# Heads 6 and 7 of the last branch in the tiles of x rows, the output's seventh operand loaded early, x rows added in the first pair, and the last addition ahead of the division

## The chip, the cores and the metric

One core of one Trainium2 chip. The time is the device time of one execution in microseconds (us). The core has five engines that run their own instruction streams: TensorE (PE in the profile, its weight loads PEld), VectorE (DVE), ScalarE (ACT), GpSimd (POOL) and SyncE (SP), which here issues nearly all DMA. An engine waits for another, or for a DMA, at a semaphore.

## What is computed

One layer that mixes 2048 tokens of width 1024 (float32), cut to its end, which is what the change touches:

```python
merged = jax.nn.sigmoid(g_a) * (y_a @ w_pa) + jax.nn.sigmoid(g_b) * (y_b @ w_pb)   # y_b: 8 heads x 128
out_x  = merged @ w_out + b_out
x      = x + gate[:, None, :] * out_x
return rmsnorm(x, g_final)
```

Ahead of it stand a projection of x, a gated convolution that gives y_a, and a bidirectional mLSTM scan of 8 heads that gives y_b.

## The kernel before

**Splits.** Every float32 factor of a large product is split in two, a high part (a cast, on ScalarE) and a low part (raw minus high, a subtraction, on VectorE). A product is three passes of matmuls: high by high, high by low, low by high. `split` (L177 to L182: the cast is L178, the subtraction L179) does it.

**Stages.** The tokens are worked on in two halves of T = 1024. At the end of the program come four branches, in this order: `w_pa` and `w_pb` for the second half, `w_pa` for the first half, beside which the last heads of the scan are finished, and `w_pb` for the first half. This text calls the last of them the last branch. A branch is eight slabs, one for each 128 columns of the weight; a slab sums 8 heads (k = 0 to 7) in three passes for two halves (j) of 512 tokens. In slab 0 both halves are run head by head; from slab 1 on one half is finished before the other. After a slab, `PbEnd.end` gates the sum (L1518), adds the part of `w_pa` on POOL (L1519) and writes it to a DRAM array `mgd` (L1520). `mgd` is read again as weights of the output.

**Heads of a branch.** `Branch.fetch` loads a head from DRAM (`ybd`) straight into the tile of its low part, lets some steps pass, and splits it there. Its `region` says where the tiles lie: region 0 takes x slots 0 to 15; region 1, which the last branch uses before the change, takes x slots 16 to 27 for heads 0 to 5 and eight small slots (`u`, `cv` in rows of the trace) for heads 6 and 7, in two halves. Heads 0 to 2 were fetched early; each later head is fetched when its scan is done.

**Output.** `output` runs eight pairs (m = 0 to 7). A pair takes 256 rows of tokens and multiplies their 1024 columns of `mgd` with `w_out` in seven products (operands o = 0 to 6 of `wod`, made earlier) into five PSUM banks, in the order X Y X W Z V Z. An operand is 12 matmuls, a pair 84. So the seventh operand uses bank Z a second time, and its first matmul must wait until the fifth operand's sum has been taken out of Z. `fin` takes sums out: into a tile `xt` of a row block of x, to which POOL has added the bias row `gb` (L1580, in `begin`), it adds an earlier part `u` (L1604) and the bank (L1605, on VectorE). For a row block with both halves, ScalarE has its squares (L1607), POOL its reciprocal root `sx` (L1611, L1613, L1614), and `close` multiplies by `sx` and the row `gf` (L1596) and writes it out. The weights of the pairs, sums of blocks of `mgd` (`sw`, made on POOL, L360), are split on the way.

The operands o = 4, 5, 6 are loaded at the start of `output` (L1626), and their six halves split inside the first pair, at steps 20, 26, 32, 40, 46 and 52 of its 84. x rows of pairs 0, 1, 2 are loaded and added to `gb` in the last branch, those of pair m + 2 at step 34 of pair m. `gb`, `gf`, and the six tiles `xt` lie in a pool `so`, which is opened where the scan's pool `sp_` is released.

**Order of the work.** TensorE's order is that of the program text. The instructions wrapped in `pin` keep their place on their engine; the other instructions of VectorE, ScalarE, POOL and SP are put in order by a scheduler. `run(...)` interleaves a stage with the queued generators `urgent` and `later`, so many steps of these for each matmul.

Of the kernel before, what the change touches and what calls it, by code (L numbers as in the profile page):

```python
# [11 lines left out]
FR = mybir.dt.float32r  # L12
# [6 lines left out]
P = 128  # L19
# [22 lines left out]
def hybrid_kernel(ctx: ExitStack, tc, x, c, ctxt, c_ctx, w_ada, b_ada, g_norm, w_in, b_in,  # L42
# [1411 lines left out]
    class Branch:  # L1454
# [11 lines left out]
        def fetch(self, k, wait=12):  # L1466
            if self.region == 0 or k < 6:
                base = 2 * k if self.region == 0 else 16 + 2 * k
                hi, lo = [xslot(base + p, [P, T], FR) for p in range(2)]
                parts = [(hi, lo, self.raw(k))]  # L1470
                for p, t in enumerate((hi, lo)):
                    for j in range(2):
                        self.t[p, k, j] = t[:, S2[j]]
            else:
                slots = [uslot] * 3 + [vslot] * 5
                parts = []
                for j in range(2):
                    hi, lo = [slots[4 * (k - 6) + 2 * j + p](FR) for p in range(2)]
                    parts.append((hi, lo, self.raw(k)[:, S2[j]]))
                    self.t[0, k, j], self.t[1, k, j] = hi, lo  # L1480
            for _, lo, raw in parts:
                ld.dma_start(lo.bitcast(F32), raw)
            yield from gap(wait)
            for hi, lo, _ in parts:
                split(hi, lo, lo.bitcast(F32), pinned=wait > 0)
# [54 lines left out]
    yb = Branch(1, lambda k: ybd[0][k], ())  # L1540
    urgent.extend(yb.fetch(k, 24) for k in ready)

    def heads_done(h):
        urgent.append(yb.fetch(h))
# [38 lines left out]
    urgent.extend(load_wo(o) for o in range(4))  # L1583
    urgent.extend(begin(m, 6) for m in range(3))
    run(branch(w_pb, yb, PbEnd, 0), 0, 0.35)
    flush(urgent)

    def output():
# [10 lines left out]
        def fin(m):  # L1599
            def f(i, j, ps, add):  # L1600
# [4 lines left out]
                nc.vector.tensor_tensor(xt[:, s], xt[:, s], ps, op=OP.add)  # L1605
# [10 lines left out]
                if m + 1 == len(tiles):  # L1616
                    close()
# [4 lines left out]
        wo.claim(range(4, 7))  # L1622
        for o in range(4, 7):
            for q in range(2):
                hi, lo = (wo.t[o][p][q] for p in range(2))
                ld.dma_start(lo.bitcast(F32), wod[wo.PLACE[o], :, 2 * q:2 * q + 2, :])  # L1626
                parts.append((hi, lo))
        for m in range(len(tiles)):
            for n, _ in enumerate(pair(st, wo, fin(m))):
                if m == 0 and n in (20, 26, 32, 40, 46, 52):  # L1630
                    hi, lo = parts.pop(0)
                    split(hi, lo, lo.bitcast(F32), pinned=True)
                if n in (10, 28):
                    close()
                if n == 34 and m > 0:
                    for _ in begin(m + 2):
                        pass
# [32 lines left out]
```

## Time and profile before

| | us |
|---|---|
| median of 3 runs | 2660.72 (2659.01 to 2660.84) |
| the profiled execution, its own time | 2660.47 |
| its span | 2658.7 |
| TensorE busy in the span | 2594.5 (98%) |
| VectorE, GpSimd, ScalarE busy | 1722.6 (65%), 1123.8 (42%), 1099.0 (41%) |
| last branch, from its first matmul to the first of the output | 2397 to 2485 of the span |

The span runs from the first to the last instruction that the profiler recorded; the time holds 1.8 us more around it. A row of a timeline gives the start, the length, the engine, the line, the operation with its tiles (out<-in), how many stand together, and in brackets the idle time of the engine ahead of it with what ended it.

### The profile page before, as it was taken

The numbers are of one execution on the slowest core, as the hardware profiler recorded it, in microseconds if no ns is written. First come the engines' busy times: TensorE is split into PE (matmuls) and PEld (weight loads), VectorE is DVE, ScalarE is ACT, GpSimd is POOL, SyncE is SP. The second block draws the span as 40 slices with busy tenths as digits, with TensorE's granted clock in tenths as the row PEclk, the third lists the DMA queues.
The fourth block names the chain that finished last, engine by engine and source line by source line (L and its number), as shares of the span: only waits on it lengthen the run. The fifth ranks groups of instructions, "written<-read, shape, count | busy, mean of one in ns | idle before, by whom it ended". The sixth has DMA issues, their size and how long they took to land.

```text
span 2658.7 us, 38177 instructions
## 1 busy us (share of the span) xinstructions
PE 2594.5 (98%) x12807; PEld 2166.7 (81%) x12807; DVE 1722.6 (65%) x3119; ACT 1099.0 (41%) x2269; POOL 1123.8 (42%) x1322
## 2 busy tenths in 40 slices
PE   8999999999999999999999999999999999999998
PEld 7788887888878787877887888888888888888777
DVE  6643237687776777478578577667666656554597
ACT  5433344333333335344443444344444544442233
POOL 1221223233345553235555555565555124422674
PEclk9999999999999999999999999999999999999999
DMA  8333344655734457435644653653566978768542
GB/s 231 101 101 106 106 139 131 211 167 179 232 118 123 139 145 236 118 100 159 195 142 130 201 160 120 195 174 128 154 195 201 301 219 273 253 194 288 195 159 96
DMA packets 373217, 452.99 MB, mean 170 GB/s; under 512 B 24428, under 2 KB 273948, under 8 KB 373020
## 3 DMA queue, kind: packets, MB, share of 16 engines
q1 hardware_dynamic: 372784, 450.46, 54.4%
q8 instruction: 102, 1.67, 0.3%
q14 instruction: 95, 0.78, 0.1%
q10 hardware_dynamic: 236, 0.08, 0.0%
HBM read 319.42 MB, written 131.03 MB: 169 GB/s over the span
## 4 chain that ended last, share of the span: by engine, by line
PE 48%; DVE 3%; DMA 2%; issue 1%; POOL 1%; ACT 0%; SPq 0%; DVEq 0%; POOLq 0%; ACTq 0%
PE pd L427 29%; PE pd L474 11%; PE pn L891 2%; PE pn L892 2%; PE pa L834 1%; PE pu L658 1%; DMA mgd<-t2k 1%; DVE wl L179 1%; PE pa L849 1%; PE pn L658 0%; PE pa L669 0%; DVE xt L1596 0%; DVE xt L1605 0%; DMA x<-wod 0%; DVE cv L999 0%
## 5 line engine op out<-in xcount | busy, mean ns | idle before, releaser
L427 PE MATMUL pd<-x,wh 128*128 128x512 f32 x5320 | 1695.9, 397 | 15.9 <-DVE xt L1605 8.5
L427 PEld LDWEIGHTS pd<-x,wh 128*128 128x128 f32 x5320 | 985.1, 189 | 209.9 <-issue 19.4
L427 PE MATMUL pd<-x,wl 128*128 128x512 f32 x2660 | 1057.3, 397 | 0.0
L427 PEld LDWEIGHTS pd<-x,wl 128*128 128x128 f32 x2660 | 501.8, 189 | 99.3 <-issue 0.2
L178 ACT CAST wh<-sw 128x512 fp32r<-128x512 f32 x382 | 237.0, 620 | 492.9 <-PE pd L427 409.0
L179 DVE TENSOR_TENSOR wl<-sw,wh 128x512 fp32r<-128x512 f32 x382 | 303.2, 795 | 182.0 <-ACT wh L178 177.1
L178 ACT CAST wh<-wr 128x512 fp32r<-128x512 f32 x350 | 216.6, 619 | 375.3 <-PE pd L427 269.9
L360 POOL TENSOR_TENSOR sw<-wr,sw 128x512 f32<-128x512 f32 x95 | 136.1, 1433 | 432.6 <-DVE wl L179 345.2
L179 DVE TENSOR_TENSOR wl<-wr,wh 128x512 fp32r<-128x512 f32 x350 | 289.7, 828 | 42.5 <-ACT wh L178 39.1
L474 PE MATMUL pd<-x,wh 128*128 128x512 f32 x896 | 281.7, 396 | 0.0
L360 POOL TENSOR_TENSOR sw<-wr 128x512 f32<-128x512 f32 x95 | 130.9, 1378 | 236.9 <-DVE wl L179 236.0
L653 POOL TENSOR_SCALAR vw<-tk,wk 128x129 f32<-128x129 f32 x205 | 161.9, 794 | 120.2 <-PE pn L658 109.7
L474 PEld LDWEIGHTS pd<-x,wh 128*128 128x128 f32 x896 | 166.3, 188 | 32.1
L474 PE MATMUL pd<-x,wl 128*128 128x512 f32 x448 | 173.4, 397 | 0.0
L186 POOL TENSOR_SCALAR ssq<-ssq 128x1 f32<-128x1 f32 x128 | 37.2, 291 | 293.7 <-ACT hf L906 289.8
L926 DVE TENSOR_TENSOR t2k<-pd,u 128x512 f32<-128x512 f32 x168 | 115.5, 688 | 59.8 <-PE pd L427 59.1
L360 POOL TENSOR_TENSOR sw<-sw,wr 128x512 f32<-128x512 f32 x94 | 132.4, 1408 | 47.9 <-DVE wl L179 37.4
L904 ACT ACTIVATE hf<-pn,rd 128x128 f32<-128x128 f32 x128 | 47.0, 367 | 246.9 <-DVE rd L900 222.4
L360 POOL TENSOR_TENSOR sw<-wr,wr 128x512 f32<-128x512 f32 x94 | 132.2, 1406 | 20.2 <-DVE wl L179 10.8
L820 POOL TENSOR_SCALAR_AFFINE_SELECT mw<-mw 128x256 f32<-128x256 f32 x128 | 61.7, 503 | 119.5 <-DMA mw<-mwd 89.1
L891 PE MATMUL pn<-tk,pt 128*128 128x129 f32 x512 | 98.8, 275 | 5.0 <-DVE hb L905 5.0
L891 PEld LDWEIGHTS pn<-tk,pt 128*128 128x128 f32 x512 | 86.8, 190 | 16.2 <-issue 5.8
(259 smaller groups left out, 3317.5 us busy)
## 6 DMA issues: line engine op xcount, KB each, us to landing
wr<-in_w_in_dram SPq DMA_DIRECT2D x176, 512.0 KB, 4.1
tk<-tokd SPq DMA_DIRECT2D x64, 386.0 KB, 3.6
mw<-mwd SPq DMA_DIRECT2D x44, 512.0 KB, 5.3
qkd<-t2k SPq DMA_DIRECT2D x64, 256.0 KB, 2.9
qk<-qkd SPq DMA_DIRECT2D x64, 256.0 KB, 3.8
tk<-tokd SPq DMA_DIRECT2D x48, 257.0 KB, 2.9
tokd<-t2k SPq DMA_DIRECT2D x32, 258.0 KB, 2.9
x<-in_w_ada_dram SPq DMA_DIRECT2D x16, 512.0 KB, 6.4
```

Source lines behind the costliest of these rows:

```text
L178: a = nc.scalar.copy(hi, raw)
L179: b = (eng or nc.vector).tensor_tensor(lo, raw, hi.bitcast(F32), op=OP.subtract)
L186: nc.gpsimd.tensor_scalar(dst, ss, 1.0 / n, EPS, op0=OP.mult, op1=OP.add)
L360: nc.gpsimd.tensor_tensor(s, a, b, op=op)
L427: nc.tensor.matmul(ps[b], op[wi][:, kk, :], xs.at(o, xi, kk), start=(fresh and kk + pi == 0), stop=(o == last[b] and kk == 3 and pi == 2), ...
L474: nc.tensor.matmul(pss[j], ops[k // 4][wi][:, k % 4, :], y(xi, k, j), start=(k + pi == 0), stop=(k == NK - 1 and pi == 2))
L653: pin(nc.gpsimd.tensor_scalar(vw, tk[:, VT], wk, None, op0=OP.mult))
L820: pin(nc.gpsimd.affine_select(mws[m][:, :, 0, d, :], mws[m][:, :, 0, d, :], pattern=[[0, 2], [s, P]], base=0, channel_multiplier=-s, compa ...
L891: nc.tensor.matmul(pn[:, d, :], pt[:, d, :], tk[:, VT], start=True, stop=False)
L892: nc.tensor.matmul(pn[:, d, :], qw[:, d, :], cur if d == carried else tk[:, ST], start=False, stop=True)
L904: nc.scalar.activation(hf, pn[:, 0, 0:P], AF.Copy, scale=rd[:, 0:1])
L926: nc.vector.tensor_tensor(t, ps, add, op=OP.add)
```

## The change

There are four edits.

1. The last branch uses a region 2. Heads 0 to 3 lie in x slots 16 to 23, heads 4 and 5 in the eight small slots, and heads 6 and 7 whole (128x1024) in tiles of the tag `xt`, that is, where x rows will lie. These two are fetched only where `so` is open, behind `gb` and `gf`.
2. With x slots 24 to 27 free, the seventh operand (o = 6) is loaded and split with operands 0 to 3 beside the last branch. In the first pair only four halves are left to split, at steps 18, 24, 32 and 40.
3. x rows: only those of pair 0 are loaded in the last branch; pair 1's at step 44 of pair 0, pair 2's at step 8 of pair 1, the others at step 36. They are stepped through `coming`.
4. In the last pair the division of a row block (`close`) is written behind the next addition of `fin`, and L1605 is pinned. The rate of the last branch's helpers is 0.36 for 0.35.

```diff
         def fetch(self, k, wait=12):
-            if self.region == 0 or k < 6:
-                base = 2 * k if self.region == 0 else 16 + 2 * k
-                hi, lo = [xslot(base + p, [P, T], FR) for p in range(2)]
+            whole = (NK, 6, 4)[self.region]
+            if k < whole or self.region == 2 and k > 5:
+                if k < whole:
+                    base = 2 * k if self.region == 0 else 16 + 2 * k
+                    hi, lo = [xslot(base + p, [P, T], FR) for p in range(2)]
+                else:
+                    hi, lo = [so.tile([P, T], FR, tag="xt", name=nm("xk"), bufs=6) for _ in range(2)]
...
-                    hi, lo = [slots[4 * (k - 6) + 2 * j + p](FR) for p in range(2)]
+                    hi, lo = [slots[4 * (k - whole) + 2 * j + p](FR) for p in range(2)]
...
-    yb = Branch(1, lambda k: ybd[0][k], ())
+    yb = Branch(2, lambda k: ybd[0][k], ())
     urgent.extend(yb.fetch(k, 24) for k in ready)
 
     def heads_done(h):
-        urgent.append(yb.fetch(h))
+        if h < 6:
+            urgent.append(yb.fetch(h))
...
-    urgent.extend(load_wo(o) for o in range(4))
-    urgent.extend(begin(m, 6) for m in range(3))
-    run(branch(w_pb, yb, PbEnd, 0), 0, 0.35)
+    last_heads = [yb.fetch(6, 6), yb.fetch(7, 1)]
+    for f in last_heads:
+        next(f)
+    urgent.extend(last_heads)
+    urgent.extend(load_wo(o) for o in (0, 1, 2, 3, 6))
+    urgent.append(begin(0, 6))
+    run(branch(w_pb, yb, PbEnd, 0), 0, 0.36)
...
-                nc.vector.tensor_tensor(xt[:, s], xt[:, s], ps, op=OP.add)
+                pin(nc.vector.tensor_tensor(xt[:, s], xt[:, s], ps, op=OP.add))
+                if m + 1 == len(tiles):
+                    close()
...
-                if m + 1 == len(tiles):
+                if m + 1 == len(tiles) and (i, j) == (0, 1):
                     close()
...
-        wo.claim(range(4, 7))
-        for o in range(4, 7):
+        wo.claim((4, 5))
+        for o in (4, 5):
...
+        coming = deque()
         for m in range(len(tiles)):
             for n, _ in enumerate(pair(st, wo, fin(m))):
-                if m == 0 and n in (20, 26, 32, 40, 46, 52):
+                if m == 0 and n in (18, 24, 32, 40):
...
-                if n == 34 and m > 0:
-                    for _ in begin(m + 2):
-                        pass
+                if (m, n) in ((0, 44), (1, 8)) or m > 0 and n == 36:
+                    coming.append(begin(len(xts), 16))
+                step(coming)
                 yield
```

In the changed file the lines below the first edit stand 4 to 11 further down: L1482 is L1486, L1580 is L1585, L1596 is L1605, L1604 and L1605 are L1613 and L1614.

The instructions move as follows. SP at the start of the last branch, before: `ybd<-g` writes head 7, the two `cv<-ybd` read it.

```order
L852 DMA ybd_135<-g_5885_23848 128x512
L252 DMA x_6023_24497<-wod 128x1024
L1503 DMA mad<-t2k_24315 128x512
L1482 DMA cv_24348<-ybd_135 128x512
L1482 DMA cv_24350<-ybd_135 128x512
L1554 DMA gb<-rowd 128x1024
L1555 DMA gf<-in_g_final_dram 128x1024
```

The same place of SP after; the tiles `xk` are heads 6 and 7.

```order
L852 DMA ybd_135<-g_5885_23848 128x512
L252 DMA x_6026_24517<-wod 128x1024
L1507 DMA mad<-t2k_24315 128x512
L1559 DMA gb<-rowd 128x1024
L1560 DMA gf<-in_g_final_dram 128x1024
L1486 DMA xk_24360<-ybd_135 128x1024
L1486 DMA xk_24363<-ybd_135 128x1024
L1517 DMA t2k_24475<-sbd_141 128x512
```

The reading loads have changed places with `gb` and `gf`, and are two whole heads instead of the halves of one.

POOL at the end of the last branch and in the first pair, before: the `t2k` rows are the branch's last gated sums, `sw` are sums of the output's weights, `sx` the first scalar operation on pair 0's rows.

```order
L1580 TENSOR_TENSOR xt_24895<-xt_24895,gb 128x1024
L1580 TENSOR_TENSOR xt_24898<-xt_24898,gb 128x1024
L1519 TENSOR_TENSOR t2k_24890<-t2k_24890,t2k_24889 128x512
L1519 TENSOR_TENSOR t2k_24930<-t2k_24930,t2k_24929 128x512
L1519 TENSOR_TENSOR t2k_24962<-t2k_24962,t2k_24961 128x512
L1519 TENSOR_TENSOR t2k_24994<-t2k_24994,t2k_24993 128x512
L360 TENSOR_TENSOR sw_25133<-wr_25027,sw_25037 128x512
L360 TENSOR_TENSOR sw_25184<-wr_25033,wr_25086 128x512
L360 TENSOR_TENSOR sw_25186<-sw_25184,wr_25033 128x512
L360 TENSOR_TENSOR sw_25233<-wr_25033 128x512
L1611 TENSOR_SCALAR sx_24811<-sx_24811 128x1
```

And after; `xt_25139` and `xt_25142` are pair 1's rows, `xt_25241` and `xt_25244` pair 2's.

```order
L1523 TENSOR_TENSOR t2k_24988<-t2k_24988,t2k_24987 128x512
L360 TENSOR_TENSOR sw_25121<-wr_25021,sw_25031 128x512
L360 TENSOR_TENSOR sw_25174<-wr_25027,wr_25074 128x512
L360 TENSOR_TENSOR sw_25176<-sw_25174,wr_25027 128x512
L1585 TENSOR_TENSOR xt_25139<-xt_25139,gb 128x1024
L1585 TENSOR_TENSOR xt_25142<-xt_25142,gb 128x1024
L360 TENSOR_TENSOR sw_25225<-wr_25027 128x512
L1622 TENSOR_SCALAR sx_24911<-sx_24911 128x1
L1585 TENSOR_TENSOR xt_25241<-xt_25241,gb 128x1024
L1585 TENSOR_TENSOR xt_25244<-xt_25244,gb 128x1024
L1622 TENSOR_SCALAR sx_24914<-sx_24914 128x1
```

Four additions of `gb` now stand among the first pair's weight sums and scalar work.

VectorE at the end of the program, before; `xt_25986` and `xt_25989` are the last pair's two row blocks.

```order
L1604 TENSOR_TENSOR xt_25989<-xt_25989,u_26342 128x512 x2
L1605 TENSOR_TENSOR xt_25989<-xt_25989,pd_26344 128x512
L1605 TENSOR_TENSOR xt_25989<-xt_25989,pd_26362 128x512
L1596 SCALAR_TENSOR_TENSOR xt_25989<-xt_25989,sx_25991,gf 128x512 x2
L1605 TENSOR_TENSOR xt_25986<-xt_25986,pd_26344 128x512
L1596 SCALAR_TENSOR_TENSOR xt_25986<-xt_25986,sx_25988,gf 128x512 x2
```

And after.

```order
L1613 TENSOR_TENSOR xt_26002<-xt_26002,u_26342 128x512 x2
L1614 TENSOR_TENSOR xt_26002<-xt_26002,pd_26344 128x512
L1614 TENSOR_TENSOR xt_26002<-xt_26002,pd_26362 128x512
L1614 TENSOR_TENSOR xt_25999<-xt_25999,pd_26344 128x512
L1605 SCALAR_TENSOR_TENSOR xt_26002<-xt_26002,sx_26004,gf 128x512 x2
L1605 SCALAR_TENSOR_TENSOR xt_25999<-xt_25999,sx_26001,gf 128x512 x2
```

The last addition of a bank stands one place earlier, ahead of the first row block's division.

## Rows read from the trace of the kernel before

**Rows 1.** Waits of TensorE, 2060 to 2659: total us, times, longest.
```profile
PE pd L427 <- DVE xt L1605: 8.5, 6, 5.0
PE pd L427 <- DVE x L179: 1.5, 2, 1.0
```

**Rows 2.** Timeline of TensorE, first pair's end and the second pair.
```profile
2498.17 0.50 PE L427 MATMUL pd<-x,wh 128*128 128x512 f32 x1 [1.01 <-DVE x L179]
...
2508.10 1.19 PE L427 MATMUL pd<-x,wh 128*128 128x512 f32 x2 [5.04 <-DVE xt L1605]
...
2512.37 0.62 PE L427 MATMUL pd<-x,wh 128*128 128x512 f32 x2
...
2529.62 0.70 PE L427 MATMUL pd<-x,wh 128*128 128x512 f32 x2 [0.75 <-DVE xt L1605]
```

**Rows 3.** Timeline of TensorE, heads 6 and 7 of slab 0, last branch.
```profile
2405.65 0.84 PE L474 MATMUL pd<-u,wh 128*128 128x512 f32 x3
...
2408.37 0.62 PE L474 MATMUL pd<-x,wh 128*128 128x512 f32 x2
```

**Rows 4.** Busy time by engine in a window, then granted clock, DMA share, GB/s.
```profile
2505.00:2508.00 3.00, 0.00 (x0) 0.00 (x0) 3.00 (x6) 0.01 (x1) 0.00 (x0) 0.50 0.52 174
```

**Rows 5.** Timeline of SP: DMA issues around the last branch.
```profile
2397.00 0.32 SPq L852 DMA_DIRECT2D ybd<-g  x1
...
2401.24 0.80 SPq L1482 DMA_DIRECT2D cv<-ybd  x2
2402.20 0.32 SPq L1554 DMA_DIRECT2D gb<-rowd  x1
...
2491.55 0.86 SPq L1626 DMA_DIRECT2D x<-wod  x2
```

**Rows 6.** DMA, 2380 to 2530: 40 slices' GB/s; issues, median us to landing.
```profile
GB/s 138 55 219 126 327 270 270 302 369 261 264 288 307 250 299 231 249 351 235 360 308 265 283 216 70 253 143 254 321 418 363 205 6 109 30 0 140 195 229 156
...
cv<-ybd SPq DMA_DIRECT2D x2, 256.0 KB, 3.4
gb<-rowd SPq DMA_DIRECT2D x1, 512.0 KB, 6.0
```

**Rows 7.** Timeline of ScalarE: a cast in the first pair.
```profile
2498.76 1.06 ACT L178 CAST x<-x 128x1024 fp32r<-128x1024 f32 x1 [0.95 <-DMA x<-wod]
```

**Rows 8.** Timeline of VectorE: last branch, first and second pair.
```profile
2413.74 1.23 DVE L179 TENSOR_TENSOR x<-x,x 128x1024 fp32r<-128x1024 f32 x1 [2.77 <-ACT x L178]
...
2499.17 0.68 DVE L1605 TENSOR_TENSOR xt<-xt,pd 128x512 f32<-128x512 f32 x1
...
2500.37 3.45 DVE L179 TENSOR_TENSOR x<-x,x 128x1024 fp32r<-128x1024 f32 x2
...
2507.28 0.67 DVE L1605 TENSOR_TENSOR xt<-xt,pd 128x512 f32<-128x512 f32 x1
...
2521.67 2.88 DVE L1604 TENSOR_TENSOR xt<-xt,u 128x512 f32<-128x512 f32 x1
```

**Rows 9.** Timeline of POOL: last branch, first and second pair.
```profile
2456.08 4.75 POOL L1580 TENSOR_TENSOR xt<-xt,gb 128x1024 f32<-128x1024 f32 x2
...
2500.53 2.21 POOL L360 TENSOR_TENSOR sw<-wr 128x512 f32<-128x512 f32 x1 [4.10 <-DVE wl L179]
...
2521.54 2.46 POOL L1580 TENSOR_TENSOR xt<-xt,gb 128x1024 f32<-128x1024 f32 x1 [1.67 <-DMA xt<-in_x_dram]
```

**Rows 10.** POOL's instructions by line, 2060 to 2659: busy, mean ns, idle ahead.
```profile
L360 POOL TENSOR_TENSOR sw<-wr,wr 128x512 f32<-128x512 f32 x8 | 10.3, 1293 | 0.2
```

**Rows 11.** Timeline of TensorE: its last matmul.
```profile
2650.16 0.39 PE L427 MATMUL pd<-x,wl 128*128 128x512 f32 x1
```

**Rows 12.** Timeline of VectorE: the end of the program.
```profile
2650.39 1.41 DVE L1596 SCALAR_TENSOR_TENSOR xt<-xt,sx,gf 128x512 f32<-128x512 f32 x2 [1.84 <-POOL sx L1614]
2651.72 0.68 DVE L1605 TENSOR_TENSOR xt<-xt,pd 128x512 f32<-128x512 f32 x1
2654.16 1.41 DVE L1596 SCALAR_TENSOR_TENSOR xt<-xt,sx,gf 128x512 f32<-128x512 f32 x2 [1.75 <-POOL sx L1614]
```

## The prediction

> **What bounds the kernel now.** I read three views in this order. The chain of waits of TensorE first, over the last branch and the output [rows 1]: in 600 us it names two causes, 8.5 us at the additions into the rows of x and 1.5 us at splits of the output's operands. Before the output nothing is waited for, so the last branch can only lose by the change, and the output can win at most 10 us plus what the clock gives back. Then TensorE's own timeline, for where these 10 us are [rows 2]: nearly all in the first pair, 1.01 us at 2498.17 and 5.04 us at 2508.10, ahead of the seventh operand's matmuls; in a later pair that wait is 0.75 us. The 12 matmuls of the seventh operand then take 2512.37 - 2508.10 = 4.27 us, where 12 undisturbed ones take 2408.37 - 2405.65 = 2.72 us [rows 3]: the granted clock had fallen to 0.50 during the wait [rows 4], the lower of its two levels, and costs 1.55 us more. Last the engines around: VectorE's timeline, for the chain of operations that ends with the L1605 waited for, and SP's and POOL's, for what the change moves; their rows are named where they are used.
>
> A change under 0.2% (5.3 us) can hardly be told from none here; that is 2655.4 to 2666.0 us. The profiled execution took 2660.47 us, 0.25 below the median of the three; the sum is made against it.
>
> **Heads 6 and 7 of the last branch.** Before, head 7 goes to spare slots: the write of that head is issued at 2397.00, its reading loads wait for the landing and go out at 2401.24, ahead of gb and gf [rows 5]; 3.4 us later they are there [rows 6], in time for slab 0, whose matmuls on heads 6 and 7 run from 2405.65 to 2408.37 without a wait [rows 3]. After, both heads go to the tiles of x rows, which exist only once the scan's pool is released. SP's order of after shows gb, gf, head 6, head 7, all behind that same write. So gb takes the place of the loads at 2401.24; with 0.3 to 0.5 us for each issue [rows 5] head 7 is issued at about 2402.6, and 2 MB stand where 0.5 MB stood.
>
> When do they land? gb alone landed 6.0 us after its issue [rows 6], at 2402.20 + 6.0 = 2408.2, while gf was on its way beside it. Cv, gb and gf are 1.5 MB, so I put the third 512 KB at about 2408.2 (head 6) and the fourth, at the 302 to 369 GB/s that the slices of this stretch show [rows 6], 1.4 to 1.7 us later: 2409.8 (head 7). Then a cast of 1.06 us [rows 7] and a subtraction of 1.23 us [rows 8]. TensorE waits for head 6's cast until 2408.2 + 1.06 = 2409.25 instead of 2405.65 (3.6 us), for head 7's low part until 2409.8 + 1.06 + 1.23 = 2412.1, and has four matmuls of 0.227 us left: slab 0 ends at 2413.0 instead of 2408.37, **4.6 us late**. Bounds: head 7 at 2408.0, no later than gb alone was, gives 2408.0 + 2.29 + 0.91 = 2411.2, 2.8 us late; if gf was not yet there at 2408.2 and two transfers follow, 1.05 MB at the 270 GB/s of the slices before it, head 7 is there at 2412.1 and the slab 6.9 us late. Nothing covers it: all later slabs queue behind slab 0 on TensorE, and they run without a wait in which the loss could be made up. A clock that falls in the wait costs between nothing and the 1.55 us above; since the wait comes in two pieces I take 0.4. Term: **+5.0**, from 2.8 to 8.5.
>
> The Trainium skill, page "SBUF — State Buffer", section "The DMA setup-cost knee", gives a transfer some 2 us plus its bytes at 436 GB/s; for 2 MB from 2401.24 that is an estimate of 6.8 us, head 7 there at 2408.1, and a slab that is about 2.9 us late. By the page's rule gb would have landed in 3.2 us; the trace has 6.0, so the measurement decides for the later landing.
>
> **The first pair of the output.** The two loads of the seventh operand, its two splits (a cast on ScalarE, a subtraction of 1.2 us on VectorE) leave the first pair for the last branch, whose TensorE has no wait and whose DMA loses 2 MB of x rows for 1 MB of operand: I cost them there at nothing; if VectorE's cover fails it is 2.4 us. In their place come x rows: of six additions of gb, which stood in the last branch, four move into the first pair, in POOL's order between the third of its weight sums and the scalar work of the row. Their loads take the place of the last two operand loads, issued at 2491.55 [rows 5], and land, as those did, just before the cast at 2498.76 [rows 7]. That is where VectorE begins its last stretch: L1605 at 2499.17, and from there to the end of the L1605 waited for (2507.28 + 0.67 = 2507.95) 8.78 us.
>
> These additions do not run beside VectorE. Where one of 2.46 us began at 2521.54, the VectorE addition of two tiles beside it took 2.88 us instead of 0.67 [rows 8, 9]; where POOL's weight sum took 2.21 us instead of 1.29 [rows 10], the two VectorE splits beside it took 3.45 us instead of twice 1.23. Operations with both inputs in SBUF take turns on the two engines; those with an input in PSUM (L1605, L441) I take as free of it. I count VectorE's at the 0.6 us by which they follow one another (two from 2499.17 to 2500.37), its subtraction at 1.15, POOL's addition at 2.35 (two of them took 4.75 at 2456.08). So the stretch after, from 2499.17 in turns: addition 2.35 (L1605 beside it), split of a weight 0.6, addition 2.35, the one subtraction that remains 1.15, weight sum 1.3 (L441 beside it), split 0.6, scalar work 0.2, L1604 0.6, addition 2.35, L1604 0.6, L1605 0.6, together 12.7 us. Against 8.78 the bank is free **3.9 us later**, though two subtractions less stand in it. If the rows land some 2 us later or the turns fall otherwise, two additions stand ahead of the bank instead of three: 3.9 - 2.35 = +1.55. I take the middle, **+2.7**. The twelve matmuls behind it keep their low clock, and the shorter waits before them go into the longer one.
>
> Without any addition in it the stretch is 12.7 - 7.05 = 5.65 us, 3.1 less than now; with the clock held that is 4.7 us won, and 7.3 if TensorE waits only the 0.75 us of a later pair (1.5 of [rows 1] at x, 5.04 and 1.55, less 0.75). This is the price of the rival below. In pairs 1 to 5 the order on VectorE and POOL stays in kind; nothing there.
>
> **The end.** The last matmul begins at 2650.16 and the last addition from PSUM should follow at 2650.6; it begins at 2651.72, since the division of the other row (two operations, 1.41 us) stands ahead of it [rows 11, 12]. After, it stands first. The division that ends the program follows its addition, and the other row's, now behind it, fits in the 1.75 us in which VectorE waits for POOL. Term: 2651.72 - 2650.6 = **-1.1**, bounds -1.4 and 0.
>
> **Sum.** 2660.47 + 5.0 + 2.7 - 1.1 = **2667.1**, say 2667; with all bounds 2663.7 (2.8, 1.55, -1.1) to 2671.8 (8.5, 3.9, -1.1).
>
> **Rivals.**
> A. The sum: late heads, three or two additions before the bank. Chance 0.45.
> B. One addition only stands ahead of the bank (1.55 - 2.35 = -0.8 for the first pair): 2660.47 + 5.0 - 0.8 - 1.1 = 2663.6. For it: two of the four belong to a later pair, and the loads can land late. Chance 0.15.
> C. The additions cost the first pair nothing: POOL does them before 2499.17 or after the bank is free. The first pair wins 4.7 to 7.3, middle 6.0: 2660.47 + 5.0 - 6.0 - 1.1 = 2658.4, not slower. The point from which it decides: no addition runs on POOL between the pair's first L1605 (2499.17) and the one that frees the bank. For it: the x rows' loads stand behind the last writes of the branch, whose own loads share the queue with 2 MB of x rows that are gone, so they may start some us earlier. Against it: POOL's order puts two weight sums ahead of them. With the heads at their lower bound it is 2656.2, and 2654.9 with the full 7.3. Chance 0.18.
> D. The change does not make slab 0 wait: the heads land by 2404.5. That needs 2 MB in 3.3 us, over 600 GB/s, where no slice of the stretch shows more than 418 [rows 6]; or a branch that starts later. 2660.47 + 2.7 - 1.1 = 2662.1. Chance 0.05; together with C's additions 2653.4, chance 0.08.
> E. Worse than A: head 7 behind other transfers beyond 2412, or splits of the operand that hold up VectorE in the branch: over 2671.8. Chance 0.09.
>
> **Numbers.** Faster by over 0.2%: the 0.08 of D with C and 0.05 of C, 0.13. Slower: E and of A what lies above 2666.0 (0.33), 0.42. Same: the rest, 0.45. The range leaves out E's top and the lower half of D with C: 2653 to 2671.5; A's own is 2663.7 to 2671.8.
>
> **What would show it.** Slab 0 of the last branch: TensorE waiting for the cast, then the subtraction, of head tiles, 3 to 5 us in all, and gb, gf, heads on SP behind the write. First pair: POOL's additions of 2.35 us between 2498 and 2512 (shifted by the 5 us), VectorE operations of 2 to 3 us beside them, the wait at the second row's L1605 of 7 to 9 us. End: the last L1605 right behind the last matmul. I am wrong if slab 0 shows under 2 us of waits, or if the wait for the bank in the first pair falls below 5 us.

## The result and the profile after

The changed kernel takes 2673.7 us (median of 4 runs, 2672.23 to 2676.84), before 2660.47 (4 runs, 2659.01 to 2660.84): a ratio of 1.0052, 95% interval 1.0035 to 1.007. That is slower by 13 us, and above the forecast range, which ended at 2671.5. A second measurement beside five rounds of before gave 2673.34 against 2662.19, a ratio of 1.0044 (1.0027 to 1.0061).

The chain of waits of TensorE from the branches on, in the changed kernel (total us, times, longest), answers to [rows 1]:

```profile
PE pd L427 <- DVE xt L1614: 7.0, 6, 4.2
PE pn L891 <- DVE hb L905: 6.0, 1, 6.0
PE pd L474 <- ACT xk L178: 3.8, 1, 3.8
PE pd L427 <- DVE x L179: 1.5, 1, 1.5
...
PE pd L474 <- DVE xk L179: 0.2, 1, 0.2
```

The two rows with xk are the forecast wait in slab 0. The row with L905 was not forecast: it is a wait of the scan. The other two causes were there before (8.5 and 1.5 us, [rows 1]); they are 7.0 and 1.5 us now, and most of both lies in the first pair.

Where the 16.4 us between the two profiled executions lie (spans 2675.1 and 2658.7) is read from TensorE's timeline. Each stage begins with its first matmul, and its length is the difference of two such starts:

| stage | before | after | difference |
|---|---|---|---|
| all up to the first half's w_pa branch | 2291.33 | 2293.37 | +2.04 |
| w_pa branch, first half (with the scan's last heads) | 106.14 | 115.02 | **+8.88** |
| last branch, slab 0 | 10.90 | 16.91 | **+6.01** |
| last branch, slabs 1 to 7 | 76.16 | 77.37 | +1.21 |
| output, first pair | 27.84 | 27.60 | -0.24 |
| pair 1 | 20.06 | 19.48 | -0.58 |
| pairs 2 to 7, to the last matmul's start | 117.73 | 117.73 | 0.0 |
| from there to the end | 8.49 | 7.63 | -0.86 |

The first line is no part of the change: over the profiled executions of this study that stretch ends between 2288.4 and 2293.4, with before's at 2291.33 and a second one of the changed kernel at 2291.60, and the profiled execution of the changed kernel was the slowest of its four.

**The w_pa branch.** Timeline of the changed kernel, ScalarE, VectorE, SP and TensorE together, in order of time:

```profile
2317.13 0.62 ACT L178 CAST wh<-wr 128x512 fp32r<-128x512 f32 x1 [1.94 <-PE pd L474]
2317.78 0.69 DVE L179 TENSOR_TENSOR wl<-wr,wh 128x512 fp32r<-128x512 f32 x1
...
2320.12 0.42 SPq L252 DMA_DIRECT2D x<-wod  x1
...
2326.24 1.05 ACT L178 CAST x<-x 128x1024 fp32r<-128x1024 f32 x1 [8.49 <-DMA x<-wod]
2327.32 1.23 DVE L179 TENSOR_TENSOR x<-x,x 128x1024 fp32r<-128x1024 f32 x1 [8.84 <-ACT x L178]
2328.46 0.68 DVE L1506 SCALAR_TENSOR_TENSOR t2k<-t2k,pd 128x512 f32<-128x512 f32 x1
...
2329.66 0.15 DVE L897 SCALAR_TENSOR_TENSOR den<-pn,em 128x2 f32<-128x2 f32 x1
...
2332.74 0.35 DVE L905 SCALAR_TENSOR_TENSOR hb<-pn,rd,hf 128x128 f32<-128x128 f32 x1 [0.52 <-ACT hf L904]
2333.15 0.80 PE L891 MATMUL pn<-tk,pt 128*128 128x129 f32 x2 [5.96 <-DVE hb L905]
```

`x<-wod` is the first half of the seventh operand. Its load is issued at 2320.12 and its cast stands next on ScalarE, which does nothing for 8.49 us until the load lands; VectorE's subtraction stands behind the cast and VectorE does nothing for 8.84 us. The scan's small operations (L897 to L905) stand behind that subtraction, and TensorE waits 5.96 us for the last of them. The busy times by engine of that wait and of the stretch behind it, with the granted clock:

```profile
2326.50:2333.20 6.70, 0.74 (x5) 0.28 (x3) 5.26 (x9) 3.74 (x6) 0.00 (x0) 0.91 0.94 287
2333.20:2339.10 5.90, 5.90 (x19) 5.02 (x20) 2.10 (x7) 2.95 (x11) 2.09 (x5) 0.53 0.78 241
```

After the wait TensorE runs 5.9 us at a mean granted clock of 0.53, so nearly all of them at the lower of its two levels (1.2 GHz). Of the 8.88 us that the branch loses, 5.96 are the wait, and the other 2.9 go to the clock.

**Slab 0 of the last branch**, the place of [rows 3, 5, 7]:

```profile
2407.92 0.32 SPq L852 DMA_DIRECT2D ybd<-g  x1
...
2412.13 0.32 SPq L1559 DMA_DIRECT2D gb<-rowd  x1
...
2412.97 0.90 SPq L1486 DMA_DIRECT2D xk<-ybd  x2
...
2419.45 2.23 ACT L178 CAST xk<-xk 128x1024 fp32r<-128x1024 f32 x2 [4.64 <-DMA xk<-ybd]
...
2420.55 1.10 PE L474 MATMUL pd<-xk,wh 128*128 128x512 f32 x2 [3.84 <-ACT xk L178]
2421.81 1.22 PE L474 MATMUL pd<-xk,wh 128*128 128x512 f32 x2 [0.16 <-DVE xk L179]
...
2425.30 0.63 PE L474 MATMUL pd<-x,wh 128*128 128x512 f32 x2
```

Head 6 is there 7.3 us after gb's issue (forecast 7.0), its cast frees TensorE after 3.84 us (3.6). The second wait of the forecast, 1.0 us for the low part of head 7, is not there: the 0.16 us are for the low part of head 6. The 12 matmuls of heads 6 and 7 take 2425.30 - 2420.55 = 4.75 us where 2.72 are needed [rows 3]; the granted clock of that stretch is 0.64:

```profile
2420.50:2425.30 4.80, 4.58 (x12) 3.18 (x13) 2.45 (x3) 2.37 (x3) 0.00 (x0) 0.64 1.07 372
```

**The first pair**, whose first matmul starts at 2502.67, in order of time; it answers to [rows 2, 8, 9]:

```profile
2505.81 2.02 SPq L1581 DMA_DIRECT2D xt<-in_x_dram  x3
...
2511.05 4.55 DVE L179 TENSOR_TENSOR x<-x,x 128x1024 fp32r<-128x1024 f32 x2
2511.38 6.48 POOL L1585 TENSOR_TENSOR xt<-xt,gb 128x1024 f32<-128x1024 f32 x2 [0.81 <-DMA xt<-in_x_dram]
2515.52 0.68 DVE L1614 TENSOR_TENSOR xt<-xt,pd 128x512 f32<-128x512 f32 x1
2516.11 2.30 DVE L179 TENSOR_TENSOR wl<-sw,wh 128x512 fp32r<-128x512 f32 x1
...
2519.61 0.50 PE L427 MATMUL pd<-x,wh 128*128 128x512 f32 x1 [1.54 <-DVE x L179]
...
2521.18 3.43 DVE L1613 TENSOR_TENSOR xt<-xt,u 128x512 f32<-128x512 f32 x2
2521.42 5.41 POOL L1585 TENSOR_TENSOR xt<-xt,gb 128x1024 f32<-128x1024 f32 x2
2524.52 0.67 DVE L1614 TENSOR_TENSOR xt<-xt,pd 128x512 f32<-128x512 f32 x1
...
2525.25 1.22 PE L427 MATMUL pd<-x,wh 128*128 128x512 f32 x2 [4.21 <-DVE xt L1614]
```

All four additions of gb are in the pair, and each VectorE operation on two SBUF tiles that begins beside one is long: 2.30 us for a split of 0.68. From the first L1614 to the end of the one waited for it is 2525.19 - 2515.52 = 9.67 us (before 8.78; forecast 12.7 with three additions in it, 10.3 with two, 11.5 in the middle). The first addition and the start of the second (2514.47) lie ahead of that stretch, and the fourth ends behind it (2526.83), so the time of about two additions lies in it.

**The end**, [rows 11, 12]:

```profile
2667.48 0.39 PE L427 MATMUL pd<-x,wl 128*128 128x512 f32 x1
...
2667.91 0.69 DVE L1614 TENSOR_TENSOR xt<-xt,pd 128x512 f32<-128x512 f32 x1 [2.03 <-PE pd L427]
2668.51 1.41 DVE L1605 SCALAR_TENSOR_TENSOR xt<-xt,sx,gf 128x512 f32<-128x512 f32 x2
2670.64 1.42 DVE L1605 SCALAR_TENSOR_TENSOR xt<-xt,sx,gf 128x512 f32<-128x512 f32 x2 [0.71 <-POOL sx L1625]
```

The last addition follows the last matmul's start after 0.43 us instead of 1.56, and the other row's division lies in the wait for POOL.

### The profile page after: what moved, and what is told of

It is laid out like the page before. It is cut to its first block, busy times and chain, and to the rows that moved or that the text cites. A ratio compares the mean times of both kernels' runs of the same rounds, so it can differ in the third digit from the quotient of the medians.

```text
span 2675.1 us, 38191 instructions
## 1 busy us (share of the span) xinstructions
PE 2602.3 (97%) x12807; PEld 2171.0 (81%) x12807; DVE 1729.1 (65%) x3119; ACT 1099.1 (41%) x2269; POOL 1127.1 (42%) x1322
## 4 chain that ended last, share of the span: by engine, by line
PE 83%; DVE 8%; DMA 4%; issue 3%; ACT 2%; POOL 1%; SPq 0%; DVEq 0%; ACTq 0%; POOLq 0%
PE pd L427 57%; PE pd L474 12%; PE pn L891 2%; PE pn L892 2%; DVE wl L179 2%; PE pc L454 2%; PE pn L658 1%; PE pa L669 1%; PE pa L834 1%; PE pu L1104 1%; PE pu L658 1%; DVE cv L999 1%; PE pd L509 1%; DVE t2k L926 1%; DMA wr<-in_w_in_dram 1%
## 5 line engine op out<-in xcount | busy, mean ns | idle before, releaser
L427 PEld LDWEIGHTS pd<-x,wh 128*128 128x128 f32 x5320 | 986.3, 189 | 208.2 <-issue 12.7
L179 DVE TENSOR_TENSOR wl<-sw,wh 128x512 fp32r<-128x512 f32 x382 | 311.2, 816 | 184.6 <-ACT wh L178 179.7
```

The lines of the kernel that those rows point to most:

```text
L179: b = (eng or nc.vector).tensor_tensor(lo, raw, hi.bitcast(F32), op=OP.subtract)
L427: nc.tensor.matmul(ps[b], op[wi][:, kk, :], xs.at(o, xi, kk), start=(fresh and kk + pi == 0), stop=(o == last[b] and kk == 3 and pi == 2), ...
```

## The experiments

Times are medians; the ratio is that to before, run beside them, with its 95% interval. The stages are read as above, in us, from one profiled execution of each kernel. They differ between executions of one program: the first pair by 1.5 us between e4 and e12, which are one kernel, and slab 0 by 1.0 between the two of the changed kernel. In the files of e1, e3 and e5 the addition of the bank (L1614) is L1621 or L1622; in e9 and e11 it is L1625, the addition of gb is L1592 and the division L1616.

| run | time, before | ratio (interval) | w_pa | slab 0 | 1 to 7 | pair 0 | pair 1 | end |
|---|---|---|---|---|---|---|---|---|
| before | | | 106.14 | 10.90 | 76.16 | 27.84 | 20.06 | 8.49 |
| changed, again (e0) | 2673.34, 2662.19 | 1.0044 (1.0027 to 1.0061) | 113.45 | 17.91 | 77.45 | 27.85 | 19.53 | 7.63 |
| e1, splits late | 2669.06, 2662.28 | 1.0021 (1.0013 to 1.003) | 106.14 | 18.05 | 77.38 | 28.47 | 19.48 | 7.63 |
| e2, heads first | 2670.29, 2662.28 | 1.003 (1.0019 to 1.0042) | 112.42 | 12.95 | 77.33 | 27.51 | 19.50 | 7.64 |
| e3, both | 2664.0, 2662.28 | 1.0008 (0.9998 to 1.0018) | 106.14 | 15.69 | 77.44 | 28.68 | 19.49 | 7.63 |
| e5, both, no additions | 2657.05, 2662.19 | 0.9977 (0.9966 to 0.9989) | 106.14 | 15.45 | 77.35 | 20.41 | 19.47 | 7.64 |
| e9, additions later | 2663.08, 2660.27 | 1.0008 (0.9999 to 1.0017) | 106.14 | 12.12 | 77.34 | 20.38 | 29.74 | 7.61 |
| e10, heads alone | 2665.92, 2660.27 | 1.0023 (1.0013 to 1.0032) | 106.14 | 15.27 | 77.36 | 20.38 | 29.27 | 7.63 |
| e11, one pair ahead | 2664.9, 2661.36 | 1.0017 (1.0007 to 1.0027) | 106.14 | 12.23 | 77.34 | 20.64 | 21.75 | 7.62 |
| e7, heads in x slots | 2668.93 (a single run) | | 106.14 | 16.26 | 77.11 | 31.90 | 19.47 | 7.64 |
| e4, last edit alone | 2660.47, 2662.28 | 0.9992 (0.9984 to 1.0001) | 106.14 | 10.88 | 76.16 | 28.56 | 19.50 | 7.62 |
| e12, the same again | 2660.94, 2661.36 | 0.9994 (0.9985 to 1.0003) | 106.14 | 10.99 | 76.17 | 30.03 | 19.47 | 7.62 |
| e8, loads by ScalarE | 2666.06, 2662.19 | 1.0013 (1.0002 to 1.0025) | 106.14 | 11.34 | 76.17 | 35.35 | 19.47 | 7.63 |

**The changed kernel again.** No edit.

> The changed kernel unchanged, beside the others. Theory (the scan's wait is part of the change): the 5.96 us wait of TensorE in the branch before the last is there again, slab 0 loses 6 us again, and the time is 11 to 14 us above that of before. Rival (that wait was an accident of one execution): no such wait, and the time is that of the run with the operand's splits kept late, about 7 us above before.

The wait is there again (5.3 us at L905), the branch takes 7.31 us more than before's, slab 0 7.01 more, and the time is 11 us above before. It was no accident of one execution.

**The operand's splits kept late (e1).** The loads stay where the change has them.

```diff
     def load_wo(o):
         wo.claim([o])
         yield
-        wo.load(wod, [o])
+        if o == 6:
+            for q in range(2):
+                hi, lo = (wo.t[o][p][q] for p in range(2))
+                ld.dma_start(lo.bitcast(F32), wod[wo.PLACE[o], :, 2 * q:2 * q + 2, :])
+                yield from gap(8)
+                split(hi, lo, lo.bitcast(F32), pinned=True)
+        else:
+            wo.load(wod, [o])
         yield from gap(20)
```

> The changed kernel with one edit: the casts and subtractions of the seventh operand keep their place in the program (behind heads 6 and 7 in the last branch) instead of standing among the scan's instructions of the branch before; its two loads stay where the change has them. Theory (the cast that waits for its load holds up ScalarE and VectorE and with them the scan): TensorE's wait of 5.96 us and the low clock behind it go, 8.9 us less, about 2664.8 us, and slab 0 still loses 6 us. Rival (the 1 MB of loads among the scan's loads is what delays it): the wait stays, 2672 to 2675 us.

The chain of waits of this kernel, over the branches and the output:

```profile
PE pd L427 <- DVE xt L1621: 6.9, 6, 3.3
PE pd L474 <- ACT xk L178: 4.2, 1, 4.2
PE pd L427 <- DVE x L179: 2.3, 1, 2.3
```

The row with L905 is gone, and the w_pa branch takes 106.14 us, that of before to the hundredth, though both loads are still issued in it. So the loads cost nothing there; the cast that waits in line for one of them cost 8.9, 7.3 and, in e2 below, 6.3 us. The time is 2669.06, not the 2664.8 expected, on a chip where before itself is 1.8 us above the first measurement and slab 0 lost 7.15.

**Heads 6 and 7 ahead of gb and gf (e2).**

```diff
-    ld.dma_start(gb_t, rowd)
-    ld.dma_start(gf_t, ...)
...
     for f in last_heads:
         next(f)
+    ld.dma_start(gb_t, rowd)
+    ld.dma_start(gf_t, ...)
```

> The changed kernel with one edit: heads 6 and 7 are loaded ahead of gb and gf. Theory (the heads are late because 1 MB stands ahead of them): head 6 is there about 4 us and head 7 about 5.2 us after the first issue instead of 7.3 and 8.5, slab 0 waits some 1 us instead of 4 and keeps its clock, 4 to 5 us less, about 2669 us. Rival (the write that they wait for and the other transfers set it): less than 1 us gained, 2673 us.

```profile
PE pn L891 <- DVE hb L905: 4.4, 1, 4.4
...
PE pd L474 <- ACT xk L178: 0.9, 1, 0.9
PE pd L474 <- DVE xk L179: 0.5, 1, 0.5
```

In this chain of waits slab 0's is 1.4 us, and the slab takes 12.95 us instead of 16.91, 4 us less, as expected. The scan's wait is still there. From e1 to e3 the same edit took only 2.4 us off the slab (18.05 to 15.69), so how much of the 6 us the 1 MB ahead of the heads was worth is shown only to within 2 to 4.

**Both edits (e3).**

> Both edits together. Theory: the gains add, 2673.7 - 8.9 - 4.8 = 2660.0 us, level with the kernel before. Rival (with the scan's wait gone the heads are late again for another reason, or the operand's splits now delay those of the heads): 2664 us or more.

2664.0 us, which is the rival's number: the interval includes before's time, but 4 us of the expected gain are missing, because the heads are late again and slab 0 still loses 4.8 us. In the kernels with the heads first it loses between 1.2 (e9) and 4.8 us (e3), although e3 and e9 issue in the same order. In e3 the heads' loads, which wait for the landing of head 7's write, are issued 4.99 us after the slab's first matmul and the first cast starts 4.5 us after that; in e9 it is 3.89 and 3.4. So each of the two landings takes about 1.1 us longer in e3. What decides that was not found; the run that issues the heads with fewer operand loads beside them (e10) did not get the loss down.

**No additions in the first pair (e5).** On e3; leaves gb out of pairs 1 and 2.

```diff
         for xt, _, _, _ in xts[m]:
-            pin(nc.gpsimd.tensor_tensor(xt, xt, gb_t, op=OP.add))
+            if m not in (1, 2):
+                pin(nc.gpsimd.tensor_tensor(xt, xt, gb_t, op=OP.add))
             yield
```

> The kernel of both edits (operand's splits late, heads ahead of gb) without the four additions of gb to the rows of pairs 1 and 2, which leaves the bias out of these 512 rows; their loads stay. Theory (these additions and VectorE's operations take turns in the first pair): the first pair falls from 28.7 us to 23 to 25, the second is unchanged, the time is 4 to 5 us below that run. Rival (the first pair is bound by the arrival of operands 4 and 5): at most 1 us less.

The first pair falls from 28.68 to 20.41 us, and its one wait is 1.03 us. So four additions cost 8.3 us there, more than the theory expected, and without them the pair is 7.4 us shorter than before's: the change's early operand does what it could do, and the additions take it all back. The kernel is faster than before by 0.2%, but it leaves the bias out and so does not compute the layer.

**The additions later (e9).** On e3: POOL's scalar work of the rows is kept in program order, and the additions stand behind it.

```diff
-                    nc.gpsimd.tensor_scalar(rs, ss[:, j:j + 1], EPS, None, op0=OP.add)
+                    pin(nc.gpsimd.tensor_scalar(rs, ss[:, j:j + 1], EPS, None, op0=OP.add))
...
                 if (m, n) in ((0, 44), (1, 8)) or m > 0 and n == 36:
-                    coming.append(begin(len(xts), 16))
+                    coming.append(begin(len(xts), {(0, 44): W1, (1, 8): 40}.get((m, n), 16)))
```

`W1` is 30. The two further operations that make `sx` are pinned in the same way.

> The kernel of both edits with the four additions of gb kept in the program and moved behind the scalar work of the first pair's rows (POOL's scalar work is kept in program order, pair 1's rows are added at step 74 of pair 0, pair 2's at step 48 of pair 1). Theory (the additions cost only where they take turns with the first pair's last stretch): the first pair takes 20.5 to 22 us as without them, pair 1 and 2 take up to 2 us more, the time is some 5 us below the run of both edits and 2 to 3 below before. Rival (they take turns with VectorE wherever they stand, which is busy nine tenths of the time in the output): what the first pair wins pairs 1 and 2 lose, and the time is that of both edits.

The timeline of POOL and VectorE in this kernel's pair 1, and TensorE's waits at the additions of the banks, of which the longest is in it:

```profile
2509.57 5.19 POOL L1592 TENSOR_TENSOR xt<-xt,gb 128x1024 f32<-128x1024 f32 x2
2512.44 4.57 DVE L1616 SCALAR_TENSOR_TENSOR xt<-xt,sx,gf 128x512 f32<-128x512 f32 x2
...
2517.02 2.85 POOL L1592 TENSOR_TENSOR xt<-xt,gb 128x1024 f32<-128x1024 f32 x1
...
2520.81 2.38 POOL L1592 TENSOR_TENSOR xt<-xt,gb 128x1024 f32<-128x1024 f32 x1
...
2526.53 2.79 POOL L1592 TENSOR_TENSOR xt<-xt,gb 128x1024 f32<-128x1024 f32 x1
```

```profile
PE pd L429 <- DVE xt L1625: 11.2, 6, 8.3
```

Five additions now stand in pair 1 ahead of the end of this wait, and a sixth begins behind it. The first pair wins 8.3 us against e3, pair 1 loses 10.25. That is the rival: VectorE's operations beside the additions are long here too, 4.57 us for the two operations of a division that take 1.41 at the end of the program.

**Heads alone on the queue (e10).** On e9; the loads of heads 6 and 7, gb, gf and operands 0 to 3 keep program order on SP.

```diff
             for _, lo, raw in parts:
-                ld.dma_start(lo.bitcast(F32), raw)
+                i = ld.dma_start(lo.bitcast(F32), raw)
+                if self.region == 2 and k > 5:
+                    pin(i)
...
```

The loads of gb, gf and the operands are pinned in the same way.

> As the run before, and the loads of heads 6 and 7, of gb, gf and of operands 0 to 3 keep their program order on SP, so that one operand load instead of three or four stands beside the heads'. Theory (what remains of slab 0's loss is the queue beside the heads): slab 0 loses 1 to 2.5 us instead of 4.8, 2 to 3 us below the run before. Rival (the write of head 7 and its landing set it): slab 0 still loses 4 us or more.

Slab 0 loses 4.37 us, the rival's number, but its cause is not the one that the rival names: the write lands earlier here, and the heads are issued 3.41 us after the slab's first matmul (3.89 in e9). It is their own loads that land late, the first cast 5.53 us after the issue (3.42 in e9), with fewer operand loads in the queue. Why stays open. The kernel is slower than the one it was made from.

**One pair ahead (e11).** On e9; two additions in each pair.

```diff
-                if (m, n) in ((0, 44), (1, 8)) or m > 0 and n == 36:
-                    coming.append(begin(len(xts), {(0, 44): W1, (1, 8): 40}.get((m, n), 16)))
+                if n == 44:
+                    coming.append(begin(m + 1, 30))
```

> As the run with the additions later, but with every pair's rows one pair ahead only: two additions in each pair, behind the scalar work of that pair's rows, none doubled. Theory (pair 1 lost 9.7 us because five additions stood in it, where a pair hides two): the first pair takes 20.4 us, pairs 1 to 6 19.5 to 20.3 us each as before, slab 0 loses 1.2 to 4.8 us as in the other runs, 2655 to 2659 us where before has 2660 to 2662. Rival (the additions come too late for the rows' first sums): pairs 1 to 6 lose 1 us or more each, and the time is above that of before.

The first pair takes 20.64 us, but pairs 1 to 6 take 19.70 to 22.72: 1.7, 1.1 and in pairs 3 to 6 together 7.0 us more than before. The times are the rival's, its cause is not: pair 1's additions end at 2512.80, and the first sum onto these rows begins only at 2520.75 on VectorE, behind operations that the additions made long (4.57 us for a division again). In the kernel before, pairs 1 to 5, with two additions each where the scheduler had put them, take 19.9 to 20.1 us, and pair 6, which has none, 19.04: there they cost about 1 us a pair at most, in a row behind the scalar work more.

**Heads in x slots (e7).** The changed kernel with heads 6 and 7 in slots 24 to 27 and the seventh operand loaded in the first pair.

```diff
-                    hi, lo = [so.tile([P, T], FR, tag="xt", name=nm("xk"), bufs=6) for _ in range(2)]
+                    hi, lo = [xslot(2 * k + 12 + p, [P, T], FR) for p in range(2)]
...
-    urgent.extend(load_wo(o) for o in (0, 1, 2, 3, 6))
+    urgent.extend(load_wo(o) for o in (0, 1, 2, 3))
...
-        wo.claim((4, 5))
-        for o in (4, 5):
+        wo.claim((4, 5, 6))
+        for o in (4, 5, 6):
...
-                if m == 0 and n in (18, 24, 32, 40):
+                if m == 0 and n in (20, 26, 32, 40, 46, 52):
```

> The changed kernel with heads 6 and 7 in x slots 24 to 27, and therefore the seventh operand loaded and split in the first pair as before; the rest as changed. Theory: no wait of the scan; slab 0 loses less than 6 us since only loads behind gb and gf are late; and if the slower slabs 1 to 7 of the change (77.4 us instead of 76.2) come from where the heads lie, they take 76.2 again. Rival: slabs 1 to 7 stay at 77.4 us.

Slabs 2 to 7 take 10.88 us each, as before; in the changed kernel each takes 11.05 (slab 1 took 11.83 here, behind the wait in slab 0). So the loss goes with the place of the heads. The rows of a slab show which matmuls are longer: six on u or cv tiles take 1.36 us in the changed kernel, six on xk tiles 1.40, and so do the six behind them, on heads 0 and 1, which lie in x slots,

```profile
2450.17 0.62 PE L474 MATMUL pd<-u,wh 128*128 128x512 f32 x2
...
2451.53 0.63 PE L474 MATMUL pd<-xk,wh 128*128 128x512 f32 x2
...
2452.93 0.63 PE L474 MATMUL pd<-x,wh 128*128 128x512 f32 x2
...
2454.33 0.62 PE L474 MATMUL pd<-x,wh 128*128 128x512 f32 x2
```

and in this kernel six on heads 6 and 7 in x slots take 1.36, and the six behind them 1.36:

```profile
2450.28 0.62 PE L474 MATMUL pd<-x,wh 128*128 128x512 f32 x2
...
2451.64 0.62 PE L474 MATMUL pd<-x,wh 128*128 128x512 f32 x2
...
2453.00 0.39 PE L474 MATMUL pd<-x,wh 128*128 128x512 f32 x1
```

**The last edit alone, on the kernel before (e4, and again e12).**

```diff
-                nc.vector.tensor_tensor(xt[:, s], xt[:, s], ps, op=OP.add)
+                pin(nc.vector.tensor_tensor(xt[:, s], xt[:, s], ps, op=OP.add))
+                if m + 1 == len(tiles):
+                    close()
...
-                if m + 1 == len(tiles):
+                if m + 1 == len(tiles) and (i, j) == (0, 1):
                     close()
```

> The kernel before with the last edit of the change alone: the last addition ahead of the division of the other row block. Theory: 0.9 to 1.1 us less, 2659.5 us, with the last addition right behind the last matmul. Rival (the division behind it ends as late): no change.

> The kernel before with the last addition ahead of the division, a second time, beside the run above on one chip. Theory: 0.9 us below before again, 2659.5 to 2661.5 us; the run above is below it if the first pair's gain exceeds slab 0's loss.

The end takes 7.61 to 7.64 us instead of 8.49 in every kernel that has this edit, about 0.87 us less. Of the other stages pair 1 is 0.6 us shorter in both executions, but the first pair is 0.7 and 2.2 us longer and pairs 2 to 7 together 0.8 and 0.6; the edit pins L1605 in every pair, but that this is the cause is not shown. From the first matmul of the w_pa branch to the end the two take 367.4 and 368.7 us, before 367.3. The medians lie 1.8 and 0.4 us below before, and both intervals include 1. So the gain at the end is shown, and a gain of the whole is not.

**The operand loads on ScalarE's queue (e8).** On e4.

```diff
-                ld.dma_start(lo.bitcast(F32), wod[wo.PLACE[o], :, 2 * q:2 * q + 2, :])
+                pin(nc.scalar.dma_start(lo.bitcast(F32), wod[wo.PLACE[o], :, 2 * q:2 * q + 2, :]))
```

> The kernel before with the last addition ahead of the division, and with the six loads of operands 4 to 6 issued by ScalarE instead of SP, where they stood behind the last writes of the last branch. Theory (the first pair's stretch is late because these loads land late): they land 3 to 6 us earlier, the waits at x vanish and that at the bank shrinks, 2 to 5 us less than before, 2656 to 2658 us. Rival (the stretch on VectorE is bound by its own operations): 1 us less than before, as with the addition alone.

ScalarE's own queue and its next cast, in this kernel:

```profile
2483.77 14.69 ACTq L1628 DMA_DIRECT2D x<-wod  x6
2498.58 0.62 ACT L178 CAST wh<-sw 128x512 fp32r<-128x512 f32 x1 [14.19 <-DMA x<-wod]
```

The six issues stand among waits, in this trace mostly for the landing of earlier transfers (`mgd<-t2k`, `t2k<-mad`, `t2k<-sbd`), and with them they hold ScalarE for 14.69 us. The copy and casts behind them wait: the first pair takes 35.35 us. Whether earlier loads alone would help it, this run doesn't tell.

## Why the prediction was wrong

The direction and the wait in slab 0 were right; the time was above the range because of one step that the sum costed at nothing. Without it, in e1, the time is 2669.06, inside the range.

1. **The step that failed**: "The two loads of the seventh operand, its two splits ... leave the first pair for the last branch, whose TensorE has no wait ...: I cost them there at nothing". They went to the branch before. Its x slots 24 to 27 have no other use there in the change, and the scheduler put the loads 50 rows ahead of gb on SP and the casts among the scan's operations on ScalarE; the tiles x_6077 and x_6079 are two of these slots:

```
L832 ACTIVATE wt_23531<-mw_23271,a_1385 128x128
L178 CAST wh_23561<-wr_23402 128x512
L178 CAST x_6077_24816<-x_6079_24818 128x1024
L178 CAST wh_23567<-wr_23402 128x512
...
L904 ACTIVATE hf_23593<-pn_23554,rd_23591 128x128
```

   This order could have been read before the result. Cost: 6.3 (e2), 7.3 and 8.9 us, shown by e1, which takes only the splits away from there and has the branch at its old length. E named "splits of the operand that hold up VectorE", but in the wrong branch and at a chance of 0.09.

2. **Late heads, +5.0** (2.8 to 8.5): measured +6.01 and, again, +7.01. The queue and the first landing were right (heads behind gb and gf, TensorE's wait for head 6's cast 3.84 us against 3.6). The second wait, 1.0 us for head 7, did not come: 0.16 us at head 6's low part was all. The clock was mis-sized: 0.4 us taken, 12 matmuls in 4.75 us instead of 2.72 measured, so 1.9 us with the 0.16 taken off. That gb and gf ahead of the heads are part of the cause is shown by e2, where the slab loses 2.05; that they are not all of it, by e3, e5 and e10, where it loses 4.4 to 4.8 with the heads first. The Trainium skill's page "SBUF — State Buffer", section "The DMA setup-cost knee", gave an estimate of 6.8 us until head 7; the trace has 7.3 us until head 6 alone, so it was too early here.

3. **Slabs 1 to 7, "they run without a wait in which the loss could be made up"**: right, but they became 1.2 us longer, which no term held (e7: it goes with where the heads lie).

4. **The first pair, +2.7** (1.55 to 3.9): measured -0.24, and 0.01 in the second execution. By the prediction's own sign it was wrong here: the wait for the bank is 4.21 us, below 5. The mechanism is shown: e5 prices the four additions at 8.3 us and the pair without them at 7.4 us less than before, the 7.3 of rival C. What failed is the landing, which the prediction put where the last operand loads had theirs, 14.2 us after the pair's first matmul (2498.76 - 2484.53). The rows' loads were issued from 3.1 us after it on (2505.81 - 2502.67) instead of 7.0 (2491.55 - 2484.53), and POOL, which waited for them, began the first addition at 2511.38, 8.7 us after it and ahead of the stretch; about two additions stand in the stretch, which is 9.67 us. The stretch itself began 12.85 us after the pair's first matmul (2515.52 - 2502.67) instead of 14.64 (2499.17 - 2484.53), which the prediction had left where it was. The number is near rival B's -0.8, but not by its mechanism, a single addition in the stretch. The Trainium skill's page "SBUF — State Buffer", section "Who interferes with whom", says that a VectorE instruction with two SBUF inputs and a GpSimd instruction that reads SBUF contend, and that the lock is exclusive; the trace agrees, 2.30 us for a split of 0.68 that begins at 2516.11, within the second addition, and ends at 2518.41, behind that addition's end (2517.86).

5. **The end, -1.1** (-1.4 to 0): measured -0.86, and -0.87 in e4 alone.

By the stages above the changed kernel without the scan's wait is 5.5 us slower than before (6.01 + 1.21 - 0.24 - 0.58 - 0.86), and e1, which is that kernel, measured 6.8 us slower. That this is near the forecast of 6.6 is luck in good part: late heads were 1 to 2 us more than forecast, slabs 1 to 7 were 1.2 more, and the first pair was 2.9 less.

No version that computes the layer was found to beat the kernel before clearly. The last edit alone takes 0.87 us off the end, and its medians are below before, but neither its timing nor its stages as a whole show a gain.

## What to carry to other kernels

An instruction that waits for a transfer costs what stands behind it on its engine, so where an edit frees space early, read on each engine where the freed work now stands: here a cast between two scan steps cost 6 to 9 us, while the loads beside it cost nothing. Work moved between two engines that take turns is not hidden because both have idle time; count what one stretch hides (two additions a pair, in their old places, for about 1 us) and expect to pay for each more wherever it stands, here 2 us each or more. Waits of 4 to 6 us on TensorE cost 1.5 to 2.9 us more at the lower clock in these traces; put that into the sum with the wait.

## What the runs showed of the hardware

With heads 6 and 7 in the xk tiles a slab takes 11.05 us instead of 10.88, at a granted clock of 1.00: 0.17 us a slab, 1.2 us a branch, in every kernel of the table that has the heads there and in none that has not. Half of it lies on the matmuls on xk, 1.40 us in sixes where the same two heads in x slots take 1.36 (e7). The other half lies on the matmuls behind them, on heads 0 to 2, although these lie in the same x slots in e7 and are not longer there. So reading the xk tiles is not the whole of it. What about the place of these tiles does it was not tried.

Six DMA issues on ScalarE, with the waits between them for earlier transfers, held the engine for 14.69 us (e8).
